# A hybrid attention/SSD layer: row spreads by DRAM round trips instead of matmuls, and GpSimd scalings with two operations

## The chip, the cores and the metric

The kernel runs on one core of a Trainium2 chip. A core has TensorE (PE, the matrix engine; PEld is its weight load), VectorE (DVE), ScalarE (ACT), GpSimd (POOL) and SyncE (SP), which issues transfers. On-chip memory has 128 partitions; matmuls write to PSUM. The metric is the time of one execution on the device in microseconds; smaller is better. All matmul inputs are 32-bit floats, and many products are taken as three matmuls of rounded halves (high by high, high by low, low by high).

## The reference

One layer works on x of 1024 rows by 1024 columns. A vector c gives six modulation vectors through `w_ada`: shift, scale and gate for the mixer (`sh_m, sc_m, g_m`) and for the FFN (`sh_f, sc_f, g_f`).

```python
h = rmsnorm(x, norm_mix_w) * (1 + sc_m) + sh_m
z, xbc, dt_raw, q, k, v = split(h @ w_in)
y_ssd = ssd_mixer(z, xbc, dt_raw, ...)       # 8 heads of 64, state 128, two B/C groups
y_att = chunk_attention(q, k, v, rel_bias)   # 8 heads, own chunk and 8 before it, softmax
x = x + g_m * (concat(y_ssd, y_att) @ w_out)
h = rmsnorm(x, norm_ffn_w) * (1 + sc_f) + sh_f
x = x + g_f * conv_ffn(h, w_up, ffn_conv_w, w_down)
return rmsnorm(x, final_norm_w)
```

Inside the SSD mixer, with `adt = dt * A` per position and head (A is negative), the decay between positions is

```python
a_cs = cumsum(adt)                        # within a chunk
seg = a_cs[:, None] - a_cs[None, :]       # for every pair (l, s) of a chunk, per head
decay_ls = exp(where(l >= s, seg, -inf))
y_diag = einsum(cb, decay_ls, X)          # cb = C B^T of the chunk
```

The table of `seg`, 128 by 128 for each of 8 heads in each of 8 chunks, is what the changed part computes. The gates `g_m` and `g_f` are the other changed part: they are needed as rows of 512 or 1024 values that are the same on all partitions. (The kernel takes SSD chunks of 128 positions; the recurrence over chunks is exact for any length.)

## The kernel before

The rows of x are eight tiles of 128. The stages are, in order: the first norm and the first projections; attention for four pairs of heads (about 99 to 290 us of the profiled execution); the projections and causal convolution of the SSD inputs, with `w_ada` columns being multiplied with c on DVE in between (`mod_col`, L134); the z projection in two halves (`z_tile`, ch 1 and then ch 0); a loop over eight SSD chunks, in which the product with `w_out` runs as well; then the FFN.

The kernel is written against a framework that adds semaphores by itself. Within an engine, instructions run in the order of the built program. That order is made by a planner, which simulates a timeline by its own costs when the program is built; where the source says `issue_after`, an instruction is tied behind another. In the SSD loop all matmuls are chained in the written order by `pe` (the line L699 is that helper's, and stands for all matmuls of the loop).

Attention (`attn_scores`): for each query tile and each of two heads, DVE adds the bias and finds the row's extremum (L413), ACT takes the exponential and the row sum (L416), DVE the reciprocal (L418), and POOL scales the tile of 128 to 640 columns by it (L419, tile `p`, eight buffers). PE then transposes the scaled tiles (L445, L448).

Gate rows: `mod_col` leaves the gates as columns, eight columns `gcol` of 128 partitions for `g_m` (L762) and eight for `g_f`. `row_of` turns eight columns into a row: four columns at a time are put on the diagonals of a 128x512 tile on DVE (L141), a matmul with a matrix of ones spreads the sums to all partitions (L144, tile `rowps`), and ACT copies them out (L145). The first half of the `g_m` row is `rowb`, which multiplies four of the `w_out` tiles on DVE (`wout_fold`, L612); the second half is `gm1`. The `g_f` row goes to DRAM as a full 128x1024 tile (`gfd`, 512 KB) and is read back as `gf` late in the FFN.

The weights of the second z half are read, rounded on ACT (`wzh`, L82) and the rest taken on DVE (`wzl`, L83). `dt_prep` follows after the first z tile of that half: some twenty small operations on 128x64 tiles make `dt` and `adt` (L667 to L680; `sm_e` holds `adt`), then `adh` and `adl`, its rounded half and rest. Three small matmuls and an exponential (L686, L687) give the cumulative decays `ea`, `de`, `cd`.

`ssd_pre(c)` prepares chunk c. For each of the two groups g of four heads: ACT and DVE build `rm`, the lower triangle `tle` times `adt` of each head, as high and low halves (L714 on ACT, L716 on DVE for the low half of g=0, L720 on ACT for g=1); two matmuls with the strict triangle `sgtr` (two records each) give `seg` in PSUM, tile `sg`; ACT takes the exponential from PSUM to `th` (L739); DVE multiplies it by the masked C B^T tile `cb` (L740). `xdt` (L707, DVE) and `xdd` (L708, POOL) are the scaled inputs. `ssd_y(c)` uses them on PE: `ydp` (diagonal part, from `th` and `xdt`), `yop` and `stp` (state). `ssd_pre(0)` runs among the z tiles; `ssd_pre(c+1)` runs within chunk c. Beside this, `wout_split` splits the `w_out` tiles to `hH` and `hL` (L85, L86, L82, L83), and ACT and DVE evacuate each z tile (L660 Tanh, L661 to `zs`). The PSUM tiles of the z half and of the loop share space, so the first `ydp` waits for the last z evacuation.

Of the kernel before, what the change touches and what calls it, by code (L numbers as in the profile page):

```python
# [26 lines left out]
PB = (2, 2, 1, 3)  # L27
# [37 lines left out]
def tile_block(ctx: ExitStack, tc: tile.TileContext, x, crep, pk, w_ada, w_first, w_ft, w_z,  # L65
# [71 lines left out]
    def row_of(cols, dst, psp, tag, bufs, ones, tmp):  # L137
        for hh in range(2):
            t = tmp()
            ps = psp.tile([P, 512], F32, tag=tag, bufs=bufs, name="rowps")  # L140
            V.tensor_tensor(t.rearrange("p (a b) -> p a b", a=4),  # L141
                            ident.unsqueeze(1).to_broadcast([P, 4, P]),
                            cols[:, 4 * hh:4 * hh + 4].unsqueeze(2).to_broadcast([P, 4, P]), ALU.mult)
            T.matmul(ps, ones, t, start=True, stop=True)  # L144
            A.activation(dst[hh], ps, AF.Copy)  # L145
# [255 lines left out]
    def attn_scores(p, i, bt):  # L401
        st, n, off, parts = s00 if p + i == 0 else scores(p, i)
        res = []
        for h in range(2):
# [14 lines left out]
            G.tensor_scalar(pv_, pv_, rr, None, op0=ALU.mult)  # L419
# [135 lines left out]
    adh = bcp.tile([P, 64], F32R, name="adh")  # L555
    adl = bcp.tile([P, 64], F32R, name="adl")
# [5 lines left out]
    sgtr = bcp.tile([P, P], F32R, name="sgtr")  # L562
# [19 lines left out]
    sgt_ = th512()[:, 0:P]  # L582
# [3 lines left out]
    G.affine_select(out=sgt_, in_=ones, compare_op=ALU.is_gt, fill=0.0, base=0,  # L586
                    pattern=[[-1, P]], channel_multiplier=1)
    V.tensor_copy(sgtr, sgt_)
    sgt = f32(sgtr)
# [37 lines left out]
    def rm512():  # L627
        return bcp.tile([P, S], F32, tag="rm", bufs=2, name="gt")[:, 0:512]
# [35 lines left out]
    def dt_prep():  # L664
# [38 lines left out]
    def ssd_pre(c, xp_, sgp_, between=None):  # L703
# [5 lines left out]
        ms_ = []  # L709
        for g in range(2):  # L710
            rm = bcp.tile([P, 2, 4, P], F32R, tag="rm", bufs=2, name="rm")
            hs = slice(c * 8 + 4 * g, c * 8 + 4 * g + 4)
            for h in range(4):
                A.activation(rm[:, 0, h, :], tle, AF.Copy, scale=f32(adh)[:, hs.start + h:hs.start + h + 1])  # L714
            if g == 0:
                V.tensor_tensor(rm[:, 1], tle.unsqueeze(1).to_broadcast([P, 4, P]),  # L716
                                f32(adl)[:, hs].unsqueeze(2).to_broadcast([P, 4, P]), ALU.mult)
# [21 lines left out]
            pin1 = A.activation(m, sg.rearrange("p (h l) -> p h l", h=4), AF.Exp)  # L739
# [16 lines left out]
    for st in range(NT):  # L756
        z_tile(1, st, wz)
        if st == 0:
            row_of(gcol[:, 0:8], (rowb[:, 0:512], gm1), pst, "tp", 2, ones, rm512)
            wout_get(0, 1, 4, 5, 2)  # L760
        if st == 2:
            V.tensor_tensor(gcol[:, 8:16], modc[:, G_F:G_F + 8], gbias[1], ALU.add)  # L762
            row_of(gcol[:, 8:16], [rowa[:, h] for h in halves], pst, "tp", 2, ones, rm512)
# [4 lines left out]
    for st in range(NT):  # L768
        z_tile(0, st, wz)
        if st == 0:  # L770
            dt_prep()
            pre0 = ssd_pre(0, tp_tile, tp_tile)
# [23 lines left out]

    def sg_tile():
        return ps2a.tile([P, 512], F32, tag="seg", bufs=PB[2], name="sg")

# [766 lines left out]
```

## Time and profile before

| | |
|---|---|
| median of three runs | 1221.77 us (1219.9 to 1223.88) |
| profiled execution | 1219.7 us; its span 1217.7 us |
| PE busy | 1167.9 us, 96% of the span |
| DVE busy | 927.8 us |
| ACT busy | 597.0 us |
| POOL busy | 199.9 us |
| granted TensorE clock, mean | 0.994 |

All times of the rows are microseconds from the start of the span. A group row gives line, engine, operation, written tile and read tiles, shape, count, then busy time and the mean ns of one, then the idle time of the engine before these and what ended it. A timeline row gives start and duration in front, and in brackets the idle time before and the releaser. A waiting row gives who waited for whom, total us, times and the longest. A transfer row gives destination, source, issuing queue, count, KB each and the median time from issue to landing.

### The profile page before, as it was taken

The numbers are of one execution on the slowest core, as the hardware profiler recorded it, in microseconds if no ns is written. First come the engines' busy times: TensorE is split into PE (matmuls) and PEld (weight loads), VectorE is DVE, ScalarE is ACT, GpSimd is POOL, SyncE is SP. The second block draws the span as 40 slices with busy tenths as digits, with TensorE's granted clock in tenths as the row PEclk, the third lists the DMA queues.
The fourth block names the chain that finished last, engine by engine and source line by source line (L and its number), as shares of the span: only waits on it lengthen the run. The fifth ranks groups of instructions, "written<-read, shape, count | busy, mean of one in ns | idle before, by whom it ended". The sixth has DMA issues, their size and how long they took to land.

```text
span 1217.7 us, 15636 instructions
## 1 busy us (share of the span) xinstructions
PE 1167.9 (96%) x5802; PEld 974.4 (80%) x5802; DVE 927.8 (76%) x1394; ACT 597.0 (49%) x1001; POOL 199.9 (16%) x174
## 2 busy tenths in 40 slices
PE   4998899989999989999999999999999999999996
PEld 3877787878878978888878888888888888888885
DVE  6846454686597678746999988988889869756986
ACT  4536454674243666676644533344334445433444
POOL 1205563672000034300000000000000000000522
PEclk9999999999999999999999999999999999999998
DMA  9722211311477201141123223322232278733443
GB/s 334 256 58 64 65 56 46 102 66 52 152 248 241 88 13 40 53 150 58 70 95 112 104 95 130 124 77 85 104 130 98 83 277 278 266 120 130 149 137 146
DMA packets 56395, 150.86 MB, mean 124 GB/s; under 512 B 5632, under 2 KB 5760, under 8 KB 54912
## 3 DMA queue, kind: packets, MB, share of 16 engines
q1 hardware_dynamic: 49264, 125.49, 30.6%
q10 hardware_dynamic: 7056, 24.38, 5.0%
q8 instruction: 45, 0.74, 0.3%
q14 instruction: 30, 0.25, 0.1%
HBM read 116.56 MB, written 29.10 MB: 120 GB/s over the span
## 4 chain that ended last, share of the span: by engine, by line
PE 80%; DVE 10%; ACT 4%; DMA 2%; issue 2%; POOL 1%; SPq 0%; POOLq 0%; DVEq 0%; ACTq 0%
PE wops L699 5%; PE dn L78 5%; PE dn L76 5%; PE dn L77 5%; PE uY L76 5%; PE uY L78 5%; PE uY L77 4%; PE uX L78 3%; PE uX L76 3%; PE uZ L77 3%; PE uX L77 3%; PE uZ L76 3%; PE uZ L78 3%; PE s L76 3%; PE s L77 2%; PE s L78 2%
## 5 line engine op out<-in xcount | busy, mean ns | idle before, releaser
L1427 POOL TENSOR_TENSOR ya<-ya,xs 128x512 f32<-128x512 f32 x4 | 17.2, 4334 | 557.7 <-ACT xs L1423 557.7
L77 PE MATMUL dn<-w 128*128 128x512 f32 x296 | 108.1, 392 | 0.0
L76 PE MATMUL dn<-w 128*128 128x512 f32 x296 | 108.1, 391 | 0.0
L419 POOL TENSOR_SCALAR p<-p,st 128x640 f32<-128x640 f32 (+4 forms) x64 | 98.8, 1558 | 43.9 <-DVE st L418 36.6
L78 PE MATMUL dn<-w 128*128 128x512 f32 x296 | 100.2, 391 | 0.2 <-DVE w L86 0.2
L76 PE MATMUL uY<-tH,w 128*128 128x512 f32 x248 | 97.2, 392 | 0.0
L77 PE MATMUL uY<-tL,w 128*128 128x512 f32 x248 | 97.0, 391 | 0.0
L78 PE MATMUL uY<-tH,w 128*128 128x512 f32 x248 | 96.9, 391 | 0.0
L85 ACT ACTIVATE w<-ya 128x1024 fp32r<-128x1024 f32 (+1 forms) x41 | 39.2, 956 | 87.5 <-PE uY L78 84.2
L699 PE MATMUL wops<-hH,yhl 128*128 128x512 f32 x224 | 74.1, 399 | 2.9 <-DVE yhl L86 1.5
L78 PEld LDWEIGHTS dn<-w 128*128 128x128 f32 x296 | 55.4, 188 | 13.3 <-DVE w L86 1.1
L76 PEld LDWEIGHTS dn<-w 128*128 128x128 f32 x296 | 55.5, 188 | 12.3
L77 PEld LDWEIGHTS dn<-w 128*128 128x128 f32 x296 | 55.5, 188 | 12.2
L85 ACT ACTIVATE w<-xs 128x1024 fp32r<-128x1024 f32 (+1 forms) x41 | 39.1, 954 | 37.3 <-PE uY L78 33.3
L78 PEld LDWEIGHTS uY<-tH,w 128*128 128x128 f32 x248 | 46.5, 188 | 10.4
L76 PEld LDWEIGHTS uY<-tH,w 128*128 128x128 f32 x248 | 46.6, 188 | 10.3
L77 PEld LDWEIGHTS uY<-tL,w 128*128 128x128 f32 x248 | 46.6, 188 | 10.2
L413 DVE CUSTOM_DVE_ANT_0 p<-s,bias 128x640 f32<-128x640 f32 (+4 forms) x64 | 40.4, 651 | 17.0 <-PE tp L445 5.2
L76 PE MATMUL s<-hH,wh 128*128 128x512 f32 x128 | 50.1, 391 | 2.4 <-DVE ct L520 2.3
L86 DVE TENSOR_TENSOR pt<-tp,pt 128x512 fp32r<-128x512 f32 (+2 forms) x72 | 41.5, 595 | 13.2 <-ACT pt L85 12.8
L699 PEld LDWEIGHTS wops<-hH,yhl 128*128 128x128 f32 x224 | 41.8, 188 | 12.2 <-DVE yhl L86 1.9
L1101 DVE SCALAR_TENSOR_TENSOR a<-cv,pkt,a 128x1023 f32<-128x1023 f32 (+1 forms) x40 | 51.1, 1279 | 0.1
(459 smaller groups left out, 3428.8 us busy)
## 6 DMA issues: line engine op xcount, KB each, us to landing
wos<-in_w_ada_dram SPq DMA_DIRECT2D x25, 512.0 KB, 4.6
gz<-a ACTq DMA_DIRECT2D x10, 1024.0 KB, 5.0
ya<-in_w_up_dram SPq DMA_DIRECT2D x11, 768.0 KB, 4.2
xs<-in_w_up_dram SPq DMA_DIRECT2D x11, 768.0 KB, 4.3
adat<-in_w_ada_dram SPq DMA_DIRECT2D x16, 512.0 KB, 5.5
raws<-in_w_ft_dram SPq DMA_DIRECT2D x14, 512.0 KB, 4.2
gy<-a ACTq DMA_DIRECT2D x10, 512.0 KB, 2.6
qk<-in_x_dram SPq DMA_DIRECT2D x8, 512.0 KB, 6.6
```

The lines of the kernel that those rows point to most:

```text
L76: T.matmul(ps, lh, rh, start=start, stop=False, skip_group_check=more)
L77: T.matmul(ps, lh, rl, start=False, stop=False, skip_group_check=more)
L78: T.matmul(ps, ll, rh, start=False, stop=stop, skip_group_check=more)
L85: i = A.activation(hi, src, AF.Copy) if ehi is A else ehi.tensor_copy(hi, src)
L86: return i, elo.tensor_tensor(lo, src, f32(hi), ALU.subtract)
L413: V.tensor_tensor_reduce(out=dst, in0=src, in1=bsl, scale=-1.0, scalar=3e38, op0=ALU.add, op1=ALU.min, accum_out=nm)
L419: G.tensor_scalar(pv_, pv_, rr, None, op0=ALU.mult)
L699: i = op(*a, **k)
L1101: V.scalar_tensor_tensor(a[:, j:S], c[:, 0:S - j], w[2 - j], a[:, j:S], op0=ALU.mult, op1=ALU.add)
L1427: G.tensor_tensor(src, src, fnr[:, halves[1]], ALU.mult)
```

## The change

1. GpSimd: the softmax scaling (L419) and the epsilon addition of `rstd` (L116) each get a second operation in the same instruction, a multiplication by 1.0.
2. Gate rows: `row_of` goes. A matmul with the identity turns the eight columns into an 8x128 tile, ACT copies it, SP writes it to DRAM (4 KB), and SP reads it back with the same rows for every partition: two reads of 128x512 for `rowb` and `gm1`, and, late, one of 128x1024 for `gf`.
3. Segment sums: in `dt_prep`, `adt` is split into a part on a fixed grid and the rest; one matmul with the triangle `tle` gives the cumulative sums of both for all 64 head-and-chunk pairs as rows (`acr`), which are written to DRAM (`acd`, 64 KB) and, transposed by PE, kept as columns (`acc`). `ssd_pre` reads, for each chunk, eight rows of each part (2 loads of 512 KB as they arrive, `cr`, in the two buffers that `rm` used), the same on all partitions. For each head DVE subtracts and adds (128x128, one instruction), ACT takes a Relu with a bias, and then, for four heads at a time, the exponential from that tile. The matmuls `sg`, the tile `sgtr`, `adh`, `adl` and `rm` go.
4. PSUM: the buffer of `sg` goes to the ring of `ydp`, `yop` and `stp`, which has four instead of three.

```diff
-PB = (2, 2, 1, 3)
+PB = (2, 2, 0, 4)
+GRID = 1.5 * 2.0 ** 17
...
-        G.tensor_scalar(ms, ms, eps, None, op0=ALU.add)
+        G.tensor_scalar(ms, ms, eps, 1.0, op0=ALU.add, op1=ALU.mult)
...
-    def row_of(cols, dst, psp, tag, bufs, ones, tmp):
-        for hh in range(2):
-            t = tmp()
-            ps = psp.tile([P, 512], F32, tag=tag, bufs=bufs, name="rowps")
-            V.tensor_tensor(t.rearrange("p (a b) -> p a b", a=4),
-                            ident.unsqueeze(1).to_broadcast([P, 4, P]),
-                            cols[:, 4 * hh:4 * hh + 4].unsqueeze(2).to_broadcast([P, 4, P]), ALU.mult)
-            T.matmul(ps, ones, t, start=True, stop=True)
-            A.activation(dst[hh], ps, AF.Copy)
+    def cols_to_dram(cols, ps, t, d):
+        T.matmul(ps, cols, ident, start=True, stop=True)
+        A.activation(t, ps, AF.Copy)
+        nc.sync.dma_start(d, t)
...
-            G.tensor_scalar(pv_, pv_, rr, None, op0=ALU.mult)
+            G.tensor_scalar(pv_, pv_, rr, 1.0, op0=ALU.mult, op1=ALU.mult)
...
+    def rows_from(d, k, n):
+        return d[k:k + n].unsqueeze(0).to_broadcast([P, n, P])
...
-        pin[:] = [i.ins for i in split(adh, adl, sm["adt"], A, V)]
+        ad, acr = (th512()[:, 0:P] for _ in range(2))
+        V.tensor_scalar(ad[:, 0:64], sm["adt"], GRID, GRID, op0=ALU.add, op1=ALU.subtract)
+        V.tensor_tensor(ad[:, 64:P], sm["adt"], ad[:, 0:64], ALU.subtract)
         dps = tp_tile()
+        T.matmul(dps[:, 192:192 + P], ad, tle, start=True, stop=True)
+        A.activation(acr, dps[:, 192:192 + P], AF.Copy)
+        nc.sync.dma_start(acd, acr)
+        T.transpose(dps[:, 320:320 + P], acr, ident)
+        V.tensor_copy(acc_, dps[:, 320:320 + P])
...
+        cr = [bcp.tile([P, 8, P], F32, tag="rm", bufs=2, name="cr") for _ in range(2)]
+        for i in range(2):
+            nc.sync.dma_start(cr[i], rows_from(acd, 64 * i + 8 * c, 8))
         for g in range(2):
-            rm = bcp.tile([P, 2, 4, P], F32R, tag="rm", bufs=2, name="rm")
-            hs = slice(c * 8 + 4 * g, c * 8 + 4 * g + 4)
             for h in range(4):
-                A.activation(rm[:, 0, h, :], tle, AF.Copy, scale=f32(adh)[:, hs.start + h:hs.start + h + 1])
-            if g == 0:
-                V.tensor_tensor(rm[:, 1], tle.unsqueeze(1).to_broadcast([P, 4, P]),
-                                f32(adl)[:, hs].unsqueeze(2).to_broadcast([P, 4, P]), ALU.mult)
-            else:
-                for h in range(4):
-                    A.activation(rm[:, 1, h, :], tle, AF.Copy,
-                                 scale=f32(adl)[:, hs.start + h:hs.start + h + 1])
-            sg = sgp_()
-            for i in range(2):
-                pe(T.matmul, sg, sgtr, rm[:, i].rearrange("p h l -> p (h l)"), start=i == 0, stop=i == 1)
+                k = 4 * g + h
+                n = 8 * c + k
+                V.scalar_tensor_tensor(cr[0][:, k], cr[0][:, k], acc_[:, n:n + 1], cr[1][:, k],
+                                       op0=ALU.subtract, op1=ALU.add)
+                A.activation(cr[0][:, k], cr[0][:, k], AF.Relu, scale=-1.0,
+                             bias=acc_[:, 64 + n:65 + n])
...
-            pin1 = A.activation(m, sg.rearrange("p (h l) -> p h l", h=4), AF.Exp)
+            pin1 = A.activation(m, cr[0][:, 4 * g:4 * g + 4], AF.Exp, scale=-1.0)
...
-            row_of(gcol[:, 0:8], (rowb[:, 0:512], gm1), pst, "tp", 2, ones, rm512)
+            cols_to_dram(gcol[:, 0:8], tp_tile()[0:8, 0:P], th512()[0:8, 0:P], gmd)
+            for t, k in ((rowb[:, 0:512], 0), (gm1, 4)):
+                nc.sync.dma_start(t.rearrange("p (a b) -> p a b", a=4), rows_from(gmd, k, 4))
             wout_get(0, 1, 4, 5, 2)
         if st == 2:
             V.tensor_tensor(gcol[:, 8:16], modc[:, G_F:G_F + 8], gbias[1], ALU.add)
-            row_of(gcol[:, 8:16], [rowa[:, h] for h in halves], pst, "tp", 2, ones, rm512)
+            cols_to_dram(gcol[:, 8:16], tp_tile()[0:8, 0:P], th512()[0:8, 0:P], gfd)
...
-    gfd = dram.tile([P, D], F32, name="gfd")
-    nc.sync.dma_start(gfd, rowa)
...
-            nc.sync.dma_start(gf, gfd)
+            nc.sync.dma_start(gf.rearrange("p (a b) -> p a b", a=8), rows_from(gfd, 0, 8))
```

More of the change, by code (lines that the diff above doesn't have):

```diff
@@ L554, in tile_block @@
     sm["nx"], sm["adt"] = sm["p"], sm["e"]
-    adh = bcp.tile([P, 64], F32R, name="adh")
-    adl = bcp.tile([P, 64], F32R, name="adl")
+    acc_ = bcp.tile([P, P], F32, name="acc")
     ex3 = bcp.tile([P, 192], F32, name="ex3")
@@ L561, in tile_block @@
     tle, ones = tle1[:, 0, :], tle1[:, 1, :]
-    sgtr = bcp.tile([P, P], F32R, name="sgtr")
+    sgt = bcp.tile([P, P], F32, name="sgt")
     wos = bcp.tile([P, 3, D], F32, name="wos")
@@ L585, in tile_block @@
                     pattern=[[1, P]], channel_multiplier=-1)
[L586 removed]
+    G.affine_select(out=sgt, in_=ones, compare_op=ALU.is_gt, fill=0.0, base=0,
                     pattern=[[-1, P]], channel_multiplier=1)
[L588 to L589 removed]
     for ft in range(4):
@@ L625, in wout_split @@
         ws[dh] += [(h[:, k:k + 512], l[:, k:k + 512]) for k in (0, 512)]
-    def rm512():
-        return bcp.tile([P, S], F32, tag="rm", bufs=2, name="gt")[:, 0:512]
+    gmd, gfd = (dram.tile([8, P], F32, name=n) for n in ("gmd", "gfd"))
+    acd = dram.tile([P, P], F32, name="acd")
+    def rows_from(d, k, n):
+        return d[k:k + n].unsqueeze(0).to_broadcast([P, n, P])
     wzp = es_t.enter_context(tc.tile_pool(name="wzp", bufs=1, side="right", reuse_waits="tile"))
```

9 lines of the change are left out of this document (3 added, 6 removed).

## The prediction

> **What bounds the kernel now.** I read the page's busy shares and chain first, then busy time by stage, then what PE waits for in each stage that the change touches.
>
> ```profile
> PE 1167.9 (96%) x5802; PEld 974.4 (80%) x5802; DVE 927.8 (76%) x1394; ACT 597.0 (49%) x1001; POOL 199.9 (16%) x174
> ```
> ```profile
> PE 80%; DVE 10%; ACT 4%; DMA 2%; issue 2%; POOL 1%; SPq 0%; POOLq 0%; DVEq 0%; ACTq 0%
> ```
>
> PE is busy for 96% of the span, and 80% of the chain is PE. So a removed matmul is worth its time, unless PE then waits. By stage (columns: stretch and length, then busy time of PE, PEld, DVE, ACT and POOL, granted clock, DMA share, GB/s):
>
> ```profile
> 99.00:290.00 191.00, 176.43 (x1026) 150.07 (x1026) 118.72 (x323) 109.08 (x253) 116.08 (x89) 0.99 0.20 64
> 427.30:510.20 82.90, 79.00 (x427) 67.61 (x428) 66.95 (x92) 56.32 (x147) 32.36 (x36) 0.98 0.09 33
> 428.00:430.00 2.00, 2.00 (x14) 1.88 (x14) 2.00 (x4) 2.00 (x5) 0.00 (x0) 0.79 0.00 0
> 430.00:432.00 2.00, 2.00 (x7) 1.58 (x6) 2.00 (x4) 2.00 (x4) 0.00 (x0) 0.50 0.00 0
> 432.00:434.00 2.00, 2.00 (x12) 1.79 (x12) 2.00 (x4) 1.82 (x6) 1.08 (x1) 0.85 0.01 4
> ```
>
> The first row is attention: PE idles 14.6 of 191 us, POOL works 116. The second is the SSD loop from the first chunk's ydp to the last's, seven periods of 11.84 us. The other three show the clock falling at its start. PE's waits in attention, and the rows around the loop's start:
>
> ```profile
> PE s L262 <- DVE st L413: 4.2, 10, 1.1
> ```
> ```profile
> PE tp L445 <- POOL p L419: 0.7, 1, 0.7
> ```
> ```profile
> 425.40 0.28 PE L78 MATMUL s<-wzh,hL 128*128 128x260 f32 x1
> 427.30 0.32 PE L699 MATMUL ydp<-xdt,th 128*128 128x64 f32 x1 [1.62 <-DVE zs L661]
> ```
>
> In attention PE seldom waits for POOL itself. Between the z products and the loop it waits 1.62 us for the last z evacuation on DVE.
>
> **Gate rows.** The four row products go:
>
> ```profile
> 387.43 0.28 PE L76 MATMUL zps<-wzh,hH 128*128 128x260 f32 x1
> 387.56 1.02 PE L144 MATMUL rowps<-gt,tle 128*128 128x512 f32 x2
> 388.01 0.68 PE L77 MATMUL zps<-wzl,hH 128*128 128x260 f32 x1
> 388.53 0.28 PE L78 MATMUL zps<-wzh,hL 128*128 128x260 f32 x1
> ```
>
> Z products start 0.12 us apart, so L78 would follow this L76 after 0.24; it follows after 1.10 with a row product (two records) between, which so costs 0.86. Four are worth 3.4 us of PE. What comes instead, two transposes of a column tile, one 128x128 product and one transpose, is small: four times 0.2 at most. But the w_out folds (L612) need the row:
>
> ```profile
> 387.22 0.16 DVE L762 TENSOR_TENSOR gcol<-modc,pkt 128x8 f32<-128x8 f32 x1
> ```
> ```profile
> 389.25 2.36 DVE L612 TENSOR_TENSOR wst<-wst,rows 128x1024 f32<-128x1024 f32 x2
> ```
> ```profile
> 392.74 1.22 DVE L612 TENSOR_TENSOR wos<-wos,rows 128x1024 f32<-128x1024 f32 x1
> ```
> ```profile
> 398.08 0.70 DVE L83 SCALAR_TENSOR_TENSOR wzl<-raws,wzh 128x520 fp32r<-128x520 f32 x1 [0.81 <-ACT wzh L82]
> ```
> ```profile
> 400.23 0.40 PE L76 MATMUL zps<-wzh,hH 128*128 128x260 f32 x2
> ```
>
> Now the column goes through a transpose and a copy (together about 1 us, an estimate), a write, and a read back of 256 KB per half, issued on SP behind the w_ada and w_out loads. Transfers, size and median us from issue to landing:
>
> ```profile
> qk<-in_w_ada_dram SPq DMA_DIRECT2D x7, 512.0 KB, 3.6
> ```
> ```profile
> xr<-in_x_dram SPq DMA_DIRECT2D x8, 512.0 KB, 4.2
> ```
> ```profile
> x1d<-xr ACTq DMA_DIRECT2D x16, 256.0 KB, 2.0
> ```
> ```profile
> dnL<-gy SPq DMA_DIRECT2D x6, 512.0 KB, 7.6
> ```
>
> With 2.0 for the write and 3.6 for the read the folds start at 387.4+1.0+2.0+3.6 = 394.0 instead of 389.25. They take 4.7 us on DVE (389.25 to 393.96), and the second z half's first weight split, wzl, stands behind them: 398.7 to 399.4. Today it ends at 398.8, and its first user on PE starts at 400.23; PE alone would be there 3.4 earlier, at 396.8, and waits until about 399.6 instead. So I keep 0.6 us of the 3.4. Bounds: 3.4 kept with a short round trip; 2 lost if the write queues on SP. gfd's write shrinks, and gf's read, late in the kernel, stays one read on SP of as much; hidden behind the w_down loads around it, it costs nothing (one landing, 4.2, if it came to be awaited). The four DVE operations L141 fall away beside other work.
>
> **Start-up of the SSD.** Before, the segment sums of chunk 0 hang on adt alone. Now adt passes through DRAM, and in the changed kernel's order on DVE the eight subtractions of chunk 1 (one per head, new) stand ahead of the last z evacuation zs, on which PE waits.
>
> ```profile
> 408.77 0.23 DVE L680 SCALAR_TENSOR_TENSOR sm_e<-sm_dt,na 128x64 f32<-128x64 f32 x1
> 408.92 1.29 DVE L707 TENSOR_TENSOR xdt<-xs,sm_dt 128x512 f32<-128x512 f32 x2
> ```
> ```profile
> 421.77 1.22 DVE L86 TENSOR_TENSOR hL<-raws,hH 128x1024 fp32r<-128x1024 f32 x1
> ```
> ```profile
> 426.82 0.43 DVE L661 SCALAR_TENSOR_TENSOR zs<-zt,s 128x260 f32<-128x260 f32 x1 [0.51 <-ACT zt L660]
> ```
> ```profile
> L714 ACT ACTIVATE rm<-tle,adh 128x128 fp32r<-128x128 f32 x48 | 15.5, 395 | 0.0
> L739 ACT ACTIVATE th<-sg 128x512 f32<-128x512 f32 x14 | 8.2, 585 | 0.0
> ```
>
> A 128x512 L707 is 0.68 and a 128x64 one 0.23, so 1 ns per element: 0.29 for 128x128, less some 0.05 of overlap: 0.25, eight are 2.0. From adt at 409.0, less the 0.6 kept, 408.4:
>
> ```profile
> GB/s 334 256 58 64 65 56 46 102 66 52 152 248 241 88 13 40 53 150 58 70 95 112 104 95 130 124 77 85 104 130 98 83 277 278 266 120 130 149 137 146
> ```
>
> - two xdt, two 128x64 operations of the split, one zs that stands between: 2.2;
> - the product stands behind z products in PE's order, half a z tile of 24x0.12 us: 1.5; copy on ACT: 0.6;
> - write of 64 KB, at the 256 KB row: 2.0;
> - two loads of 512 KB at once, 4.2 and 1.6 more (512 KB at 334 GB/s, the highest of the row below): 5.8;
> - first subtraction to last exponential of chunk 0: 0.3, eight Relu at 15.5/48 = 0.32, two exponentials of 0.585: 4.1. Only then is the buffer free for chunk 1's first load;
> - that load: 4.2;
> - chunk 1's subtractions, with two of the hL operations among them (1.13 apart), then zs: 2.0+2.3+0.4 = 4.7.
>
> Sum 25.1: the loop starts at 433.5 instead of 427.3, **+6.2**, while PE is out of work for some nine us. Bounds: +1.9 (no wait for PE's turn, loads of 3.6, both landing together) and +13 (loads of 7.6, twice 3.4 more). The rows of the clock show 0.42+1.0+0.30 = 1.7 us lost already after 1.62 us of idling; a longer idle can lose as much again or nothing: I take **+1.0** (0 to 1.7). In the Trainium skill, "TensorE: Matmul & The Clock Gate", Part 1, the clock halves after an idle window of about 3.4 us and needs about that long of work to return. The rows here show 0.50 after a shorter pause; by the page alone the longer pause would cost about 1.7 us.
>
> **The SSD loop.** Removed per chunk: two sg products.
>
> ```profile
> 449.96 0.62 PE L699 MATMUL sg<-rm,sgtr 128*128 128x512 f32 x2
> 450.42 0.39 PE L699 MATMUL wops<-hH,yhl 128*128 128x512 f32 x1
> ```
> ```profile
> L716 DVE TENSOR_TENSOR rm<-tle,adl 128x512 fp32r<-128x512 f32 x6 | 8.3, 1386 | 0.0
> ```
>
> A product is 0.46 us; 14 in the loop are 6.4 us of PE, 79.0 to 72.6, or 10.4 per period. DVE gains 56 subtractions, 14 us, and loses L716 (8.3 us): 66.95 to 72.7, also 10.4 per period. ACT loses one operation of three (32 of 96). So PE's gain meets a DVE as full as itself, whose subtractions stand in order ahead of the th product that ydp needs and now wait for a load. 0 is what I get if DVE takes it all, -6.4 if none: I take **-3.0**. A load is hidden if exponential, load and subtractions (4.1+4.2+2.0 = 10.3) fit in a period; at 7.6 us they don't (13.7), and each period grows by 1.9. The loads also stand on SP, where a load that waits for the exponentials holds back the x rows' loads behind it; those have most of a period to spare, and cost a landing's 4.2 per chunk at the worst. The segment sums' PSUM buffer goes to the ring of ydp, yop and stp, for which nothing waits today: 0.
>
> **GpSimd's two operations.** The work is the 64 scalings L419 in attention; L116's sixteen are small.
>
> ```profile
> L419 POOL TENSOR_SCALAR p<-p,st 128x640 f32<-128x640 f32 x32 | 63.8, 2010 | 6.0 <-DVE st L418 5.2 <-PE pv L457 0.8
> ```
> ```profile
> L708 POOL TENSOR_TENSOR xdd<-xdt,ex 128x512 f32<-128x512 f32 x8 | 8.8, 1100 | 156.2 <-ACT ex L687 128.7 <-PE stp L699 22.3 <-DVE xdt L707 5.2
> L419 POOL TENSOR_SCALAR p<-p,st 128x512 f32<-128x512 f32 x8 | 13.1, 1647 | 11.0 <-DVE st L418 11.0
> ```
>
> No row has two operations. The nearest is the same instruction with one, and at its price attention stays: **0**. A two-input product of 512 columns takes 1100 against 1647, so the scaling could be a third shorter: 116 us of POOL would be 83; but PE idles 14.6 us in all and names POOL for 0.7, so at most about 4 us come back. Doubled, POOL would need 215 us in a stage of 191: +24. The Trainium skill's "GPSIMD Engine Reference", section 3.1, has up to two operations per element bound by the ports at 1.03 cycles, and 1.8 cycles at 1.2 GHz for a good loop, so an estimate of 0.96 us for 640 columns; the one-operation row is twice that. By it the sum would be 4 us lower.
>
> **Sum.** 6.2+1.0-3.0+0 = +4.2 on the profiled 1219.7 us (span 1217.7): 1223.9. The median of the runs, 1221.77, stands 2.1 above that execution, so the forecast is **1226.0**. A change under 0.3%, 3.7 us, can't be told from none.
>
> **Rivals.**
> - Short loads, which decides for faster: all sixteen loads read 4 KB that every partition shares. If one lands in 2.0 us like the x1d row, start-up shrinks by 3.8+2.2 to about +0.2, the loop keeps its -6.4, the clock +1.0, the folds give another 1.6: -6.8, 1215. It turns at a landing near 3 us. For it: the memory's side is small. Against: 512 KB still go into the core, and no load row is under 3.6.
> - Cheaper scaling, -4 in attention: +0.2, 1222; with the loop at -6.4 it reaches 1218.6.
> - Slow loads: 7.6 us gives 6.8 more at start-up and 6x1.9 more in the loop for the 3 saved: 1226+6.8+14 = 1247; at 5.5 two landings are 1.3 later each and the loop's 3 are gone, 1232. For it: the row dnL, and one small source read 128 times.
> - Dearer scaling: at 1.4 times, POOL has 156 of 191 us, and each tile's softmax is 0.8 longer: PE's waits on p and pt grow, up to half of the 24 of a doubling: 1238.
>
> **How the numbers follow.** Forecast's case 0.44 (1221 to 1231: slower 0.25, same 0.15, faster 0.04); short loads 0.19 (faster 0.15, same 0.04); cheaper scaling 0.18 (faster 0.08, same 0.10); slow loads 0.11 and dearer scaling 0.08, slower. Faster 0.27, same 0.29, slower 0.44. The range, 1213 to 1240, reaches over the short loads and the dear scaling and leaves out the tail of the slow loads.
>
> **What would show it.** After: no rowps and no sg rows; DVE zs as the releaser of the first ydp after eight or more idle us of PE, with chunk 1's subtractions just ahead of it, released by a DMA; a clock of 0.5 after it; the loop from first to last ydp near 80 us; L612 starting some 5 us later; the scaling row near 2010. I am wrong if the scaling moves much, if cr loads land far from 4.2, or if PE finds other work in the gap.

## The result, and the profile after

The changed kernel takes 1224.43 us (median of 20 runs, 1220.26 to 1227.36) against 1221.28 for the kernel before, measured beside it: a ratio of 1.0023, with a 95% interval of 1.0013 to 1.0034. By the ratio that is 2.8 us slower: under the 0.3% that the prediction set as its own bound for telling a change, but with the interval above 1. The forecast was 1226.0. The profiled execution took 1222.64 us with a span of 1220.9, 3.2 longer than the span before.

Busy times of the whole, from the page of the changed kernel:

```profile
PE 1163.9 (95%) x5769; PEld 972.2 (80%) x5769; DVE 935.4 (77%) x1447; ACT 590.1 (48%) x967; POOL 149.5 (12%) x174
```

PE is busy for 4 us less and the kernel is 3 us longer: PE waits more. POOL lost a quarter of its busy time. Busy time by stage (columns as before; the first two rows answer to those of attention and of the loop from the first ydp to the last chunk's, the third is the gap ahead of the loop):

```profile
99.00:290.00 191.00, 178.11 (x1036) 152.58 (x1035) 120.12 (x324) 111.87 (x257) 63.11 (x88) 0.98 0.20 64
430.82:512.64 81.82, 76.91 (x398) 65.96 (x399) 71.79 (x135) 50.69 (x121) 33.15 (x35) 0.92 0.33 115
421.40:430.80 9.40, 0.03 (x1) 0.00 (x0) 9.14 (x15) 9.40 (x17) 3.57 (x2) 0.64 0.36 117
```

In the gap PE does nothing, while DVE and ACT are busy throughout. The loop's mean clock fell from 0.98 to 0.92. What PE waited for from 415 to 520 us (who, for whom, total, times, longest), and the rows at the gap's two ends:

```profile
PE ydp L701 <- DVE zs L656: 9.4, 1, 9.4
PE wops L701 <- DVE yhl L87: 2.7, 1, 2.7
PE ydp L701 <- DVE th L738: 1.5, 1, 1.5
```
```profile
421.15 0.28 PE L79 MATMUL s<-wzh,hL 128*128 128x260 f32 x1
430.82 0.47 PE L701 MATMUL ydp<-xdt,th 128*128 128x64 f32 x1 [9.38 <-DVE zs L656]
```

The wait for the last z evacuation grew from 1.62 to 9.38 us. In the loop PE waited in the kernel before as well, 1.43 and 1.50 us for yhl and 0.33 for th; now it waits 0.68 and 2.69 for yhl and 1.53 for th. The kernel before:

```profile
446.02 0.50 PE L699 MATMUL wops<-hH,yhl 128*128 128x512 f32 x1 [1.43 <-ACT yhl L85]
448.26 0.73 PE L699 MATMUL wops<-hH,yhl 128*128 128x512 f32 x2 [1.50 <-DVE yhl L86]
```

DVE in and ahead of the gap, in order of time:

```profile
403.83 0.22 DVE L675 SCALAR_TENSOR_TENSOR sm_e<-sm_dt,na 128x64 f32<-128x64 f32 x1
...
416.13 3.03 DVE L719 SCALAR_TENSOR_TENSOR cr<-cr,acc 128x128 f32<-128x128 f32 x8 [3.12 <-DMA cr<-acd]
...
422.34 3.71 DVE L87 TENSOR_TENSOR hL<-wst,hH 128x1024 fp32r<-128x1024 f32 x2 [0.26 <-ACT hH L86]
425.97 1.14 DVE L719 SCALAR_TENSOR_TENSOR cr<-cr,acc 128x128 f32<-128x128 f32 x4
427.03 1.22 DVE L87 TENSOR_TENSOR hL<-wos,hH 128x1024 fp32r<-128x1024 f32 x1
428.16 1.13 DVE L719 SCALAR_TENSOR_TENSOR cr<-cr,acc 128x128 f32<-128x128 f32 x4
429.21 1.22 DVE L87 TENSOR_TENSOR hL<-raws,hH 128x1024 fp32r<-128x1024 f32 x1
430.35 0.41 DVE L656 SCALAR_TENSOR_TENSOR zs<-zt,s 128x260 f32<-128x260 f32 x1
```

This is the predicted chain row by row: adt (L675), the wait for the loads, the subtractions of chunk 0, then chunk 1's subtractions between the hL operations, and behind them the evacuation zs for which ydp waits. Only the load of chunk 1 doesn't show as a wait of DVE. Issued at 421.38, it landed 4.5 us later, just when DVE ended two hL operations (at 426.05). These had taken 1.73 and 2.06 us, where the same ones took 1.22 each in the kernel before; POOL was running yy beside them:

```profile
421.40 3.57 POOL L808 TENSOR_TENSOR yy<-xs,pkt 128x512 f32<-128x512 f32 x2 [3.96 <-PE s L78]
```

The new or changed operations by themselves, from the groups of POOL, the subtractions' line (ns, shortest, median, longest) and the transfers:

```profile
L415 POOL TENSOR_SCALAR p<-p,st 128x640 f32<-128x640 f32 x32 | 28.3, 891 | 21.7 <-DVE st L414 19.4 <-PE pv L452 1.5 <-PE s L258 0.6
```
```profile
L719 DVE SCALAR_TENSOR_TENSOR cr<-cr,acc x64: 336/340/1129, 416.1 to 502.9; 128x128 f32<-128x128 f32 x64
```
```profile
cr<-acd SPq DMA_DIRECT2D x16, 512.0 KB, 3.7
```

The scaling with two operations takes 891 ns where the one with a single operation took 2010. A load of 4 KB to all partitions lands in 3.7 us, no slower than other loads of 512 KB.

### The profile page after: what moved, and what is told of

Its sections match the earlier page's. It is cut to its first block, busy times and chain, and to the rows that moved or that the text cites. A ratio compares the mean times of both kernels' runs of the same rounds, so it can differ in the third digit from the quotient of the medians.

```text
span 1220.9 us, 15671 instructions
## 1 busy us (share of the span) xinstructions
PE 1163.9 (95%) x5769; PEld 972.2 (80%) x5769; DVE 935.4 (77%) x1447; ACT 590.1 (48%) x967; POOL 149.5 (12%) x174
## 4 chain that ended last, share of the span: by engine, by line
PE 66%; DVE 7%; DMA 2%; issue 1%; ACT 1%; POOL 1%; POOLq 0%; SPq 0%; DVEq 0%; ACTq 0%
PE dn L79 5%; PE dn L77 5%; PE dn L78 5%; PE wops L701 5%; PE uY L77 4%; PE uY L79 4%; PE uY L78 4%; PE uX L79 3%; PE uZ L78 3%; PE uX L77 3%; PE uX L78 3%; PE uZ L77 3%; PE uZ L79 3%; PE s L77 2%; PE s L78 2%; PE s L79 2%
## 5 line engine op out<-in xcount | busy, mean ns | idle before, releaser
L415 POOL TENSOR_SCALAR p<-p,st 128x640 f32<-128x640 f32 (+4 forms) x64 | 46.1, 726 | 76.6 <-DVE st L414 66.4
L77 PEld LDWEIGHTS uY<-tH,w 128*128 128x128 f32 x248 | 46.5, 188 | 10.3
```

Of the source, the lines that this page charges most:

```text
L77: T.matmul(ps, lh, rh, start=start, stop=False, skip_group_check=more)
L415: G.tensor_scalar(pv_, pv_, rr, 1.0, op0=ALU.mult, op1=ALU.mult)
```

## The experiments

Every time below is a median; the time of the kernel before, in parentheses, and the ratio with its interval come from the same chips and times.

### One part at a time

The GpSimd change alone, on the kernel before:

```diff
-        G.tensor_scalar(ms, ms, eps, None, op0=ALU.add)
+        G.tensor_scalar(ms, ms, eps, 1.0, op0=ALU.add, op1=ALU.mult)
...
-            G.tensor_scalar(pv_, pv_, rr, None, op0=ALU.mult)
+            G.tensor_scalar(pv_, pv_, rr, 1.0, op0=ALU.mult, op1=ALU.mult)
```

> The kernel before with only the GpSimd change (two operations in one instruction in the softmax scaling and in rstd). The changed kernel's trace has the scaling of 640 columns at 891 ns instead of 2010 and the z products starting 2.3 us earlier. If that is all the scaling's doing (theory), this kernel is 1.5 to 2.5 us faster than before, 1219 to 1220, with the scaling row near 0.9 us, POOL's wait rows in attention smaller and the SSD loop untouched. Rival: PE's waits in attention don't hang on POOL, and the 2.3 us come from a different order of instructions there: then within 0.7 us of before. Second rival: all of PE's idle time that names DVE after the scaling goes too: 4 us faster.

Measured: 1217.55 us (1220.69), ratio 0.9964 [0.9950, 0.9979], 4.4 us faster. The price is the cause and not something else in the changed kernel: the group row of this kernel shows the same duration, and in attention POOL now stands waiting for DVE.

```profile
L419 POOL TENSOR_SCALAR p<-p,st 128x640 f32<-128x640 f32 x32 | 28.2, 887 | 21.6 <-DVE st L418 19.3 <-PE pv L456 1.5 <-PE s L262 0.6
```

The size fits the second rival better than the theory, though not its wording: PE's wait for the extremum on DVE (L413), 4.2 us before, is 1.1 here. That wait named DVE, and it fell with no edit but POOL's, so it hung on POOL, most likely by way of the tiles that POOL held. The z products start 4.4 us earlier than before (344.0 against 348.4).

The gate rows alone, on the kernel before (`row_of` replaced by `cols_to_dram` and the reads, as in the change):

```diff
-            row_of(gcol[:, 0:8], (rowb[:, 0:512], gm1), pst, "tp", 2, ones, rm512)
+            cols_to_dram(gcol[:, 0:8], tp_tile()[0:8, 0:P], th512()[0:8, 0:P], gmd)
+            for t, k in ((rowb[:, 0:512], 0), (gm1, 4)):
+                nc.sync.dma_start(t.rearrange("p (a b) -> p a b", a=4), rows_from(gmd, k, 4))
```

> The kernel before with only the gate rows through DRAM. Theory: four row products of 0.86 us go, the w_out folds start some 5 us later than before and hold back the weight splits of the second z half, so that of 3.4 us one to two are kept: 1 to 2 us faster, 1219.5 to 1220.5, with the first ydp earlier by about as much. Rival: the folds' wait is covered in full, 3.4 us faster. Other rival: the wait costs as much as the products, no change.

Measured: 1219.47 us (1220.69), ratio 0.9989 [0.9978, 1.0000], 1.3 us faster, so of 3.4 us of row products more than half is given back, as the theory had it. The interval touches 1.

The segment sums alone (the changed kernel with the row products and the one-operation scalings put back):

```diff
-            G.tensor_scalar(pv_, pv_, rr, 1.0, op0=ALU.mult, op1=ALU.mult)
+            G.tensor_scalar(pv_, pv_, rr, None, op0=ALU.mult)
...
-            cols_to_dram(gcol[:, 0:8], tp_tile()[0:8, 0:P], th512()[0:8, 0:P], gmd)
+            row_of(gcol[:, 0:8], (rowb[:, 0:512], gm1), pst, "tp", 2, ones, rm512)
```

> The kernel before with only the segment sums through DRAM (row products and one-operation scalings as before). Theory: this part alone is the loss, and more than the whole change: idle time of PE ahead of the first ydp of 8 to 10 us instead of 1.6, a granted clock of 0.5 for some 6 us after it, and a loop that gives back 2 to 3 us: 5 to 7 us slower than before, 1226 to 1229. Rival: the three parts interact (for one, the late folds delay the chain of adt), and this part alone costs no more than the whole change, 3 us.

Measured: 1227.38 us (1220.69), ratio 1.0058 [1.0039, 1.0078], 7.1 us slower. The whole loss is here, and PE's wait ahead of the loop is the same as in the full change:

```profile
PE ydp L708 <- DVE zs L663: 9.5, 1, 9.5
```

The two other parts together, without the segment sums:

```diff
-            G.tensor_scalar(pv_, pv_, rr, None, op0=ALU.mult)
+            G.tensor_scalar(pv_, pv_, rr, 1.0, op0=ALU.mult, op1=ALU.mult)
...
-            row_of(gcol[:, 8:16], [rowa[:, h] for h in halves], pst, "tp", 2, ones, rm512)
+            cols_to_dram(gcol[:, 8:16], tp_tile()[0:8, 0:P], th512()[0:8, 0:P], gfd)
```

> The kernel before with the GpSimd change and the gate rows through DRAM, and the segment sums by matmuls as before: what is left of the change without its losing part. Theory: the parts add, 4.4 and 1.3 us from the runs of each alone: 5 to 6 us faster than before, 1215 to 1216. Rival: the scaling has already moved the z stage to where it waits for DMA or DVE, and the rows add nothing: 1216.5 to 1217.5.

Measured: 1216.49 us (1220.91), ratio 0.9962 [0.9948, 0.9977], 4.6 us faster. The rows add 0.2 us to the scaling's 4.4, within the intervals: the rival. Of the kernels that compute everything, this has the lowest ratio, level with the scaling alone within the intervals; it is faster than the kernel before and than the changed one.

### The start-up: which work stands where

Chunk 1's subtractions tied behind the last z evacuation, in the changed kernel:

```diff
-                V.scalar_tensor_tensor(cr[0][:, k], cr[0][:, k], acc_[:, n:n + 1], cr[1][:, k],
-                                       op0=ALU.subtract, op1=ALU.add)
+                with tc.issue_after(zlast[1]) if c == 1 else ExitStack():
+                    V.scalar_tensor_tensor(cr[0][:, k], cr[0][:, k], acc_[:, n:n + 1], cr[1][:, k],
+                                           op0=ALU.subtract, op1=ALU.add)
```

> The changed kernel with the eight subtractions of chunk 1 tied behind the last z evacuation, on which the first ydp waits; nothing else is tied. Theory: those subtractions hold back the loop's start. But four hL operations still stand ahead of the evacuation, 1.2 us or more each, so PE idles 6 to 7.5 us instead of 9.4 and the time falls by 2 to 3 us, to 1221.5 to 1222.5. Rival: the wait moves to the th products of chunk 1 or to yhl, and the time stays at 1224.

Measured: 1218.56 us (1220.69), ratio 0.9984 [0.9969, 0.9999]. That is 0.39% under the changed kernel's ratio, 4.8 us, more than expected: the gap shrank as predicted, and the loop became shorter as well (first ydp to the last chunk's: 79.4 us instead of 81.8).

```profile
PE ydp L701 <- DVE zs L656: 7.3, 1, 7.3
```

What shortened the loop shows in the order on DVE, which the planner changed there too. In the changed kernel, five subtractions stand ahead of yhl, and PE waits 2.69 us for it (first two rows); in this run yhl stands ahead of the subtractions (last two rows), and the wait is 0.42.

```profile
449.01 2.20 DVE L719 SCALAR_TENSOR_TENSOR cr<-cr,acc 128x128 f32<-128x128 f32 x5
451.14 0.68 DVE L87 TENSOR_TENSOR yhl<-xs,yhl 128x512 fp32r<-128x512 f32 x1
```
```profile
447.97 0.93 DVE L87 TENSOR_TENSOR yhl<-xs,yhl 128x512 fp32r<-128x512 f32 x1
...
452.08 2.18 DVE L720 SCALAR_TENSOR_TENSOR cr<-cr,acc 128x128 f32<-128x128 f32 x8
```

Next, the first four w_out splits (hL on DVE, hH on ACT) were tied behind the last z evacuation too, and, as a control, the same was done in the kernel before:

```diff
-        if st == 3:
-            for j in (0, 1, 2):
-                wout_split(j, wt[j])
-            wout_get(7)
-            wout_split(3, wt[3])
+    pin[:] = zlast
+    for j in (0, 1, 2):
+        wout_split(j, wt[j])
+    wout_get(7)
+    wout_split(3, wt[3])
```

> The changed kernel with chunk 1's subtractions and also the first four splits of w_out (the hL operations on DVE and their ACT halves) tied behind the last z evacuation. Theory: the first ydp then waits only for chunk 0's own segment sums; it starts near 423 instead of 430.8 and PE idles some 2 us there. The splits are late now, and the first w_out products of chunk 0 wait for them some 3 to 5 us, so of 8 us about 5 stay: 1218 to 1220. Rival: all 8 stay, 1215 to 1216. Second rival: the wait just moves to the w_out products, 1222 to 1224.

> The kernel before with the first four w_out splits tied behind the last z evacuation: the control for the same order without the change. Theory: there PE waited 1.6 us for that evacuation and the clock fell after it; the wait goes, but the w_out products of chunk 0 wait for their splits: within 2 us of before, either sign. Rival: the order alone is worth 3 us or more to any kernel, and the gain of the reordered changed kernel is no sign of the DRAM round trip.

Measured: 1228.38 us (1220.91), ratio 1.0059 [1.0035, 1.0082], and for the control 1229.16 us, 1.0063 [1.0044, 1.0081]. Both lose: the theory fell in both, and the second rival fell short as well. The first ydp starts at 420.5 with a wait of only 1.0 us, and then PE waits for yhl, which stands behind the splits on DVE and ACT. PE's waits of the reordered changed kernel from 415 to 520 us:

```profile
PE wops L701 <- DVE yhl L87: 10.4, 2, 7.5
PE wops L701 <- ACT yhl L86: 6.8, 2, 6.1
```

So the splits must be done somewhere between the sums and the first w_out products. In the kernel before DVE did them ahead of the loop with PE still at the z tiles; both kernels tie them behind chunk 0's exponentials and th products, and in the changed kernel these come late (th ends at 422.1 and the last z product at 421.4; before, at 418.1 and 425.7).

The reading was tested the other way: the splits tied to an earlier point, the ACT copy of the cumulative sums (and the fourth z evacuation), so that they fill the time of the round trip (with chunk 1's subtractions late, as above, and the later splits behind chunk 0's th):

```diff
-        A.activation(acr, dps[:, 192:192 + P], AF.Copy)
+        pin[:] = [A.activation(acr, dps[:, 192:192 + P], AF.Copy).ins]
...
+            pinc = list(pin)
...
         if st == 3:
+            pin[:] = [pinc[0], zlast[1]]
             for j in (0, 1, 2):
                 wout_split(j, wt[j])
             wout_get(7)
             wout_split(3, wt[3])
+            pin[:] = pin0
...
-                    pin[:] = zlast
+                    pin[:] = [zlast[1], pin0[1]]
```

> The changed kernel with the first four w_out splits no longer tied behind chunk 0's exponentials, but behind the ACT copy of the cumulative sums and the fourth z evacuation; the later four behind chunk 0's th products; chunk 1's subtractions behind the last z evacuation. Theory: DVE and ACT stood still while the sums went through DRAM (DVE 3.1 us ahead of chunk 0's subtractions) and then did the splits with PE waiting; now the splits fill that time, the first ydp starts near 423 to 425 instead of 430.8, with no wait of more than 3 us ahead of the first w_out products: 6 to 8 us faster than the changed kernel, 1215 to 1218. Rival: start-up is bounded by the sum of DVE's and ACT's work there, not by its order, and the wait moves: 1221 to 1224.

Measured: 1218.13 us (1221.95), ratio 0.9977 [0.9967, 0.9988]: 5.6 us under the changed kernel's ratio, but only 0.9 under the run with late subtractions alone. The gap shrinks. DVE does the splits while the sums are on their way, and the first ydp starts at 424.9 after a wait of 4.6:

```profile
409.00 2.35 DVE L87 TENSOR_TENSOR hL<-wst,hH 128x1024 fp32r<-128x1024 f32 x2
...
411.47 1.22 DVE L87 TENSOR_TENSOR hL<-wos,hH 128x1024 fp32r<-128x1024 f32 x1
412.60 1.22 DVE L87 TENSOR_TENSOR hL<-raws,hH 128x1024 fp32r<-128x1024 f32 x1
...
415.00 3.82 DVE L720 SCALAR_TENSOR_TENSOR cr<-cr,acc 128x128 f32<-128x128 f32 x8 [0.58 <-DMA cr<-acd]
```

Of the 4.6 us won there against the run with late subtractions alone, most is lost in the loop, whose first ydp to the last chunk's takes 82.4 us against 79.4: PE waits 2.0 us for yhl there instead of 0.4. Theory and rival share this one: the start-up came as the theory had it, and the wait moved.

### The loop: loads or subtractions

The low part of the cumulative sums left out: one load per chunk, no subtraction, and the sums rounded to the grid (the output lacks that part):

```diff
-        cr = [bcp.tile([P, 8, P], F32, tag="rm", bufs=2, name="cr") for _ in range(2)]
-        for i in range(2):
-            nc.sync.dma_start(cr[i], rows_from(acd, 64 * i + 8 * c, 8))
+        cr = bcp.tile([P, 8, P], F32, tag="rm", bufs=2, name="cr")
+        nc.sync.dma_start(cr, rows_from(acd, 8 * c, 8))
...
...
-                V.scalar_tensor_tensor(cr[0][:, k], cr[0][:, k], acc_[:, n:n + 1], cr[1][:, k],
-                                       op0=ALU.subtract, op1=ALU.add)
-                A.activation(cr[0][:, k], cr[0][:, k], AF.Relu, scale=-1.0,
-                             bias=acc_[:, 64 + n:65 + n])
+                A.activation(cr[:, k], cr[:, k], AF.Relu, scale=-1.0, bias=acc_[:, n:n + 1])
```

> The changed kernel without the low part of the cumulative sums: one load of 512 KB per chunk instead of two, no subtraction on DVE, and the Relu takes the high part alone; the sums are then rounded to the grid and the low part is left out of the computation. Theory: DVE bounds the SSD loop of the changed kernel in the periods that last 11.9 us; without 64 subtractions (22 us of DVE in all) every period falls to PE's own 10.1 us, and the loop from first to last ydp to 71 to 74 us from 81.8; the start-up shrinks by the second load and the subtractions, 4 to 6 us. Together 10 to 14 us faster than the changed kernel: 1210 to 1214. Rival: the loads or the chain exponential to th bound the loop, and it stays above 78 us: 1217 to 1220.

Measured: 1213.08 us (1220.91), ratio 0.9929 [0.9909, 0.9949]: 11.5 us under the changed kernel's ratio. Start-up and loop both shrink, each by somewhat less than expected: first ydp at 428.1, 2.7 us earlier, loop 75.0 us, the last five periods at 10.1. But two things went with the edit, the subtractions and the second load. So both loads were kept, the second one read by nothing, and only the subtractions and the low part left out; the edit against the changed kernel:

```diff
-                V.scalar_tensor_tensor(cr[0][:, k], cr[0][:, k], acc_[:, n:n + 1], cr[1][:, k],
-                                       op0=ALU.subtract, op1=ALU.add)
-                A.activation(cr[0][:, k], cr[0][:, k], AF.Relu, scale=-1.0,
-                             bias=acc_[:, 64 + n:65 + n])
+                A.activation(cr[0][:, k], cr[0][:, k], AF.Relu, scale=-1.0, bias=acc_[:, n:n + 1])
```

> The kernel without the subtractions and the low part, but with both loads of each chunk kept (the second is read by nothing), into the same two buffers. It tells the subtractions' time on DVE from the loads'. Theory: DVE is what bounds the loop of the changed kernel, and the loads of 3.7 us are hidden: periods stay at 10.1 us, loop 75 to 78 us as without the load, 1213 to 1215. Rival: the loads, with two buffers and the wait for the exponentials, are what stretches it: two periods of 11.9 us come back and the time is 1217 to 1220.

Measured: 1218.25 us (1221.95), ratio 0.9980 [0.9969, 0.9991]. The rival: a load that nobody reads costs 6.2 us by the ratios, and the long periods are back (loop 80.1 us). Finally, with all computed and the late subtractions, the low part got a buffer of its own from chunk 1 on:

```diff
-        cr = [bcp.tile([P, 8, P], F32, tag="rm", bufs=2, name="cr") for _ in range(2)]
+        cr = [bcp.tile([P, 8, P], F32, tag="rm", bufs=2, name="cr"),
+              (sp_[0].tile([P, 8, P], F32, tag="crl", bufs=1, name="crl") if c else
+               bcp.tile([P, 8, P], F32, tag="rm", bufs=2, name="cr"))]
```

> The kernel with chunk 1's subtractions behind the last z evacuation, and from chunk 1 on a buffer of its own for the low part, so that the high parts alternate between two buffers; nothing is left out. In the run that kept both loads and left out the subtractions, two periods of 11.9 us stayed, and without the second load none did: with two buffers for two tiles, the loads of chunk c+1 wait for the exponentials of chunk c, and what stands behind them on ACT and DVE is late. Theory: this buffer wait is most of what holds the loop; with it gone the loop shrinks by 3 to 5 us from that kernel's 79.4, and the time is 1214 to 1216. Rival: with the subtractions on DVE the loop is held by DVE as well, and no more than 1.5 us come: 1217 to 1219.

Measured: 1221.42 us (1220.86), ratio 1.0002 [0.9989, 1.0014], 2.2 us over the kernel without the extra buffer: theory and rival both missed (loop 83.8 us). One period of each of four kernels, by windows (columns as above); first the changed kernel's long one, then the low part's own buffer, then loads without subtractions, then neither:

```profile
478.70:490.57 11.87, 10.35 (x58) 8.79 (x59) 11.87 (x24) 8.46 (x22) 4.88 (x5) 1.00 0.46 147
```
```profile
477.25:489.12 11.87, 10.36 (x59) 8.79 (x58) 11.87 (x24) 8.46 (x22) 4.88 (x5) 1.00 0.48 146
```
```profile
484.85:496.68 11.83, 10.36 (x58) 8.79 (x59) 6.43 (x11) 7.10 (x19) 4.43 (x5) 1.00 0.44 136
```
```profile
472.76:482.87 10.11, 10.11 (x60) 8.86 (x58) 8.88 (x13) 7.33 (x19) 4.56 (x5) 1.00 0.33 104
```

PE ends each of the first three with a wait of 1.5 us for th. In the first two DVE is busy for all of the 11.87 us: it bounds these periods. In the third DVE is busy for 6.43 of 11.83, and still the period is as long: there the loads hold it (with two tiles in two buffers, SP issues chunk c+1's load only after chunk c's exponentials, and ACT stood 7.8 us in all waiting for such loads). So there are two limits of about the same height, and taking the subtractions away alone left the other; in this place only the kernel with neither runs at PE's 10.11. The wait costs more than itself: the changed kernel's next period is as long without any wait, because the clock is down in it.

```profile
490.57:502.44 11.87, 11.87 (x59) 10.02 (x59) 10.05 (x22) 7.19 (x19) 5.84 (x7) 0.86 0.32 120
```

The own buffer did not test the load limit cleanly: SP still held high-part loads back behind low-part ones, for 11.3 us in all by its waits, and another period grew longer (a wait of 2.7 us for th at 442). What a full prefetch would bring with the subtractions kept wasn't tried and stays open.

The early splits were also put into the kernel without the low part:

> The same early splits in the kernel without the low part of the cumulative sums (left out of the computation: no subtraction, one load per chunk). Theory: the two gains add, since one is start-up and the other the loop: some 5 us under the 1213 of that kernel, 1207 to 1210. Rival: without the subtractions start-up has less to gain, 1211 to 1213.

Measured: 1213.03 us (1221.95), ratio 0.9939 [0.9926, 0.9953], no faster than without them (0.9929): at the edge of the rival's range, though not for its reason. The gap stayed at 7.8 us, because the planner put eight Relus of the next chunk, which wait for a load, ahead of the last z evacuation on ACT:

```profile
425.04 0.37 ACT L655 ACTIVATE zt<-s 128x260 f32<-128x260 f32 x1
426.31 2.44 ACT L718 ACTIVATE cr<-cr,acc 128x128 f32<-128x128 f32 x8 [0.90 <-DMA cr<-acd]
428.66 0.36 ACT L655 ACTIVATE zt<-s 128x260 f32<-128x260 f32 x1
```

It is the same fault as chunk 1's subtractions on DVE, on another engine.

## Why the prediction was right, and where its terms were off

The direction and the size held, and the mechanism at the start-up was the right one. Two terms were mis-sized: attention, whose gain was put at nothing, and the clock, whose loss was put at 1.0 us and came to 4.8. That the sum still came within 1 us of the span measured is in part luck, for these two errors point opposite ways.

- **Start-up, +6.2.** The chain from adt to the first ydp was put at 25.1 us and measures 26.8 (adt ends at 404.05, ydp starts at 430.82). Its parts: the two loads 5.5 (410.63 to 416.13) for 5.8; the first subtraction to the last exponential 5.2 for 4.1, because the first subtractions were slower and two z evacuations (zt) stood between on ACT; the stretch of the second load 4.6 for 4.2, with hL operations of the same length beside it; the last stretch 4.8 for 4.7. It began 4.9 us earlier than before (404.05 against 409.0), instead of 0.6, so ydp came at 430.8 and not at 433.5. 2.3 of the 4.9 came from attention; the rest from the z stage. PE's idle time was forecast at nine and is 9.38.
- **Gate rows, 0.6 of 3.4 kept.** The prediction, and the account of the kernel before, took the column written at L762 (387.22) for the one that the folds need. It is that of `g_f`. The column of `g_m` is written at L748 (L746 in the changed kernel), some 60 us ahead of its use:

```profile
L748 DVE TENSOR_TENSOR gcol<-modc,pkt x1: 169/169/169, 325.5 to 325.5; 128x8 f32<-128x8 f32 x1
```
```profile
L746 DVE TENSOR_TENSOR gcol<-modc,pkt x1: 166/166/166, 323.2 to 323.2; 128x8 f32<-128x8 f32 x1
```
```profile
391.41 2.36 DVE L604 TENSOR_TENSOR wst<-wst,rows 128x1024 f32<-128x1024 f32 x2 [3.74 <-DMA gm<-gmd]
```

  What starts the trip is the place of the matmul in PE's order: 387.56 for the row product before, 384.76 for the one with the identity now. From there to the first fold it was 1.7 us and is 6.65, and the prediction's own parts of the trip give 6.6 (1.0+2.0+3.6). So the length of the trip was right, and its start right only by luck. The folds start 2.2 later than before, or 4.5 counted from the start of the z products, where 4.75 was forecast; DVE waited 3.74 for the row. With the column there so early, the trip might have been started sooner; that wasn't tried. The part alone kept 1.3.
- **GpSimd, 0.** This is the term that failed. The nearest row, the same instruction with one operation, was taken as the price, and the two-operation form is less than half of it, 891 against 2010 ns. The prediction's rival of cheaper scaling had a third off and at most 4 us; alone the edit gave 4.4. Within the changed kernel the z products start 2.3 us earlier (346.1 against 348.4); why not the 4.4 of the edit alone stays open. The prediction had named the scaling row moving much as a sign of being wrong, and here it was. The ground given for the cap, that PE names POOL for only 0.7 us, was a bad one: the wait for the extremum that fell from 4.2 to 1.4 named DVE.
- **Clock, +1.0.** Measured by the first two windows below: from 430.82, its first product, to 437.6 PE ran at half speed, a loss of 3.4 us where the kernel before lost 1.7. So +1.7 there, the upper bound given; the full clock is back some 6.8 us after the first product. The Trainium skill's "TensorE: Matmul & The Clock Gate", Part 1, which the prediction cited, has about 3.4 us of sustained work for that; the trace has about twice as long, and by the page the loss would have been 1.7, an estimate (half of 3.4). Here the measurement decides.

```profile
431.00:437.00 6.00, 6.00 (x25) 5.64 (x26) 6.00 (x10) 3.92 (x9) 0.00 (x0) 0.50 0.38 124
437.00:438.00 1.00, 1.00 (x6) 0.92 (x5) 1.00 (x3) 0.00 (x0) 0.98 (x1) 0.68 0.80 279
448.00:459.00 11.00, 7.87 (x31) 6.20 (x32) 8.11 (x17) 5.64 (x15) 3.51 (x4) 0.84 0.21 78
487.00:498.00 11.00, 9.47 (x49) 7.91 (x48) 9.18 (x19) 7.28 (x17) 5.22 (x6) 0.84 0.40 144
```

  The last two windows hold what no term had: the clock fell again after the waits of 2.69 and 1.53 us, for another 1.4 and 1.7 us of loss. In all the loop of this execution lost 6.5 us to the clock against 1.7 before: +4.8. The length of a wait alone doesn't tell whether it costs clock. The kernel before (first row) kept a clock of 1.00 from 440 to 460, around its waits of 1.43 and 1.50 us, and the run with the GpSimd edit alone (second row), with the same two waits, did not; what decides it stays open.

```profile
440.00:450.00 10.00, 6.92 (x38) 5.63 (x39) 8.04 (x12) 5.70 (x16) 4.21 (x5) 1.00 0.01 2
```
```profile
440.00:450.00 10.00, 7.07 (x26) 5.25 (x24) 6.17 (x10) 5.37 (x13) 4.66 (x5) 0.71 0.00 1
```

- **Loop, -3.0.** The stretch went from 82.90 to 81.82, so -1.1 with the clock in it. It came about in another way than forecast. Counted at full clock, PE's busy time fell by 6.9 us (79.00 less 1.7, to 76.91 less 6.5), where 6.4 were forecast. PE's idle time rose by 1.0 (3.9 to 4.9), and the clock took 4.8, of which 1.7 is the term above. Without that the loop gave back 2.8, for 3.0 forecast: the size is right, but of the 4.1 taken back, 3.1 went through the clock, after two waits that DVE caused (for yhl behind five subtractions, and for th at the end of the 11.87 us period, in which DVE is as full as forecast). Missed as well was the load limit of the same height, which the prediction had worked out (10.3 us of a period) and called hidden.

Sum over the profiled executions: z products' start -2.3, to their end another 1.9 earlier, the gap 7.8 longer, which puts the first ydp at +3.5 where +6.2 was forecast; loop -1.1, where loop and clock together were put at -2.0; after the loop +0.8, where nothing was: +3.2 of span, against +4.2. The gain of 2.3 in attention, which was not forecast, is most of what the first ydp came earlier than forecast. The price of a subtraction was 0.34 us, not 0.25. The rivals of short and of slow loads are out: 3.7 us median.

## What to carry to other kernels

When a value makes a round trip through memory, the cost is not only the transfer but also everything that the order of work has tied behind its arrival on in-order engines; list what stands behind the first consumer, and move work that doesn't need the value ahead of it, without moving it behind something else that needs it. Change one part at a time before judging a bundle: here one part of three lost 7.1 us and the other two together gained 4.6. A wait that names one engine may hang on another that frees its buffers, so the time by releaser is no upper bound of what a faster engine brings.

## What the runs showed of the hardware

On GpSimd a tensor-scalar instruction with two operations is over twice as fast as with one: 891 against 2010 ns for 128x640, 799 against 1647 for 128x512, though the second operation multiplies by one. The gain shrinks with the size: 375 against 608 ns for 128x128, and none for a single column (the epsilon addition, median 339 against 281). In the Trainium skill, "GPSIMD Engine Reference", section 3.1, a good loop takes 1.8 cycles per element at 1.2 GHz, 0.96 us for 640 by an estimate; the two-operation form comes close to that (0.89) and the one-operation form is twice it.

A load of the same 4 KB to all 128 partitions, 512 KB in all, landed in 3.7 us median (3.3 to 5.3), like a load of 512 KB of distinct data.

A DVE subtraction of 128x128 took 0.34 us, and up to 1.13 us while POOL ran xdd (415.34 to 417.44, the time of the first subtractions). The hL operations of 128x1024 took 1.73 and 2.06 us while POOL ran yy, and 1.22 without.
